# Loading attention heads over 128 partitions: three transfers a head in place of six

## The chip, the cores and the metric

The kernel runs on one core of one Trainium2 chip. The metric is the device time of one execution in microseconds (us); the time before is the median of three runs. All times from a trace are counted from the first instruction of its one profiled execution.

## The reference

One layer of a decoder: a normalised input is projected to queries, keys, values and a pooling input; 8 attention heads and 4 pooling groups are computed side by side; their outputs are projected and added; a gated MLP with a short convolution and a gated embedding follow. Sequence 2048, model width 1024, everything in 32-bit floats. The change concerns the attention alone. Of it, cut to what is computed:

```python
N_ATT_HEADS, HEAD_DIM = 8, 64
DIL_PATTERNS = ((128, 1), (512, 4), (2048, 16))      # window, dilation
for window, dil in DIL_PATTERNS:                      # banded attention in each residue class
    s = q . k  - slope[h] * distance                  # masked to the band
    m = max(s); e = exp(s - m); den = sum(e)
    o = (e . v) / den
w = den * exp(m - max over patterns); w = w / sum(w)  # mixture of the three patterns
att = sum over patterns of w * o
```

## The kernel before

**Stages.** The program runs through three functions: `phase_project` (0 to about 400 us), `phase_attention` (about 397 to 724 us) and `phase_rest` (output projection, MLP, embedding, to the end). The order on TensorE (PE) is written out by hand throughout; in the projection and the attention so are those on ScalarE (ACT), VectorE (DVE) and GpSimd (POOL). The queue of SyncE (SP), which issues most transfers, follows the order in which the program text meets them.

**High and low parts.** Each 32-bit factor is held as the sum of two parts, a high one (name ends in h) and a low one (l), which TensorE multiplies in its fast 32-bit form. A query times a key is q_high·(k_high + k_low) + q_low·(k_high + k_low). The kernel takes both key parts in one product: a head has 64 components, so a tile of 128 partitions holds the key's high parts in 64 partitions and its low parts in the other 64 (tile `ks`), and the query tile holds its 64 components twice (tile `qhh` for the high part, `qll` for the low). The sum over the 128 partitions is then the sum over components and over both key parts. Which partition holds which component is free, as long as `ks`, `qhh` and `qll` agree.

**What the projection leaves.** `phase_project` writes queries and keys to DRAM, per pair of heads 128 rows (component) by 2048 (token) of 4 bytes, so 8 KB a row: `g.qh`, `g.ql` (L370 to 371) and `g.kh`, `g.kl` (L376 to 377), and the values to `g.vn` and `g.vf` (L391).

**The attention's order.** It takes 128 steps `s`, 16 for each head (one for each block of 128 queries). `CFG["ord"]` lists what a step records and how many steps late each piece is: scores by TensorE (`near_scores` L566, `far_scores` L555; near is a block with its predecessor, far the dilated patterns), their maxima by VectorE (`near_max` L575, `far_max` L581, which read the bias tiles `nb` and `fb`), exponentials by ScalarE, a transpose, the split into high and low, and the product with the values some 6 steps later (`near_pv` L619, `far_pv` L638). `halves_sum` (L654) adds the two halves of a result: ScalarE copies one (`ev`, L659), VectorE adds (`s`, L660), and TensorE's next product `o` (L628, L642) reuses the accumulator only then.

**Head loads.** `load_qk(h)` (L500) makes head `h`'s tiles, two sets in turn by `h % 2`, and lists its transfers. Head 0's are issued at once, then the eight value tiles of pair 0 (L738 to 742). From step 1 of each head on, the next head's list is put into `queue` and one transfer is issued at each step (L749 to 753); value tiles of the next pair are issued at fixed steps in between (`V_STEPS`). A transfer first waits until the last reader of its buffer is done. For the queues of SP and ACT together, eight semaphores are used in turn, so a transfer also waits until the one eight places before it has landed.

**Mixing the patterns.** Each pair of heads ends with a mix of its patterns. In the next head, an even one, come: the pair's maxima and sums are transposed and copied (`mix_stats` L761), stored to DRAM from ScalarE's own queue one step later (`mix_stats_store`: `std` L776, `stf` L777, 32 KB each), loaded again in another layout three steps after that, from the same queue (`mix_stats_load`: `sn` L784, `sf` L788; each must wait until the store that it reads has landed), and five steps later VectorE combines them (`mix_lift` L862). From there GpSimd goes on by itself: it stores the weights (`wd`, L880), loads them spread over 128 partitions (`wb`, L891, 24 loads), multiplies (L901 to 914) and stores the result. The last pair is mixed without DRAM.

Of the kernel before, what the change touches and what calls it, by code (L numbers as in the profile page):

```python
# [11 lines left out]
F32R = mybir.dt.float32r  # L12
# [5 lines left out]
P = 128  # L18
D = 1024
KD = D // P  # L20
S = 2048
H = 8
DH = 64
# [31 lines left out]
def rdma(nc, dst, src):  # L55
    nc.sync.dma_start(fp(dst) if dst.dtype == F32R else dst, fp(src) if src.dtype == F32R else src)
# [113 lines left out]
def phase_project(tc, g, xT, w_in, pool_w, rcnt):  # L170
# [4 lines left out]
    with ExitStack() as ctx:  # L175
# [116 lines left out]
        for c, (t0, n) in enumerate(chunks):  # L292
            cs = slice(t0, t0 + n)
            final = c == len(chunks) - 1
            nxt = None
            for gi, grp in enumerate((0, 1, 2, 3) if not final else (0, 1, 3, 2)):
                if gi == 2 and not final:
                    tk.later(2, lambda st=nxt: scale(st))
                    tk.later(5, lambda st=nxt: spread_(st))
                nt = 4 if grp != 2 else n // P  # L300
                ps = [psum.tile([P, CH], F32, tag="b1", name=f"z{c}_{grp}_{j}") for j in range(nt)]
                apart = final and grp == 2
                for k in range(KD if not apart else 0):
                    if gi == 0 and c == 0 and k < KD - ACFG["nk"]:
                        norm_b(cur, k + ACFG["nk"])
                        cur.low()
                    ahead(step + ACFG["la"])
                    step += 1
                    wh, wl = held[grp, k]
                    ah, al = cur.hn[k]  # L310
                    for j in range(nt):
                        js = slice(j * P, (j + 1) * P)
                        if grp == 2:
                            mm3(nc, ps[j], ah[:, js], al[:, js], wh, wl, k == 0, k == KD - 1)
                        else:
                            mm3(nc, ps[j][:, :n], wh[:, js], wl[:, js], ah, al, k == 0, k == KD - 1)
                    tk.tick()
                    if gi == 0 and k == 6 and not final:
                        nxt = loads(c + 1)
                    if gi == 1 and not final:  # L320
                        square(nxt, k)
                    if gi == 3 and not final:
                        if k > 1:
                            nxt.low()
                        norm_a(nxt, k)
                        if k > 0:
                            norm_b(nxt, k - 1)
                    if gi == 0 and c == 0:
                        if k < 4:
                            square(cur, 2 * k)  # L330
                            square(cur, 2 * k + 1)
                        if k == ACFG["sc"]:
                            scale(cur)
                        if k == KD - 1:
                            spread_(cur)
                            inv = nxt.xs[0][:, n : 2 * n]
                            nc.scalar.copy(inv, cur.inv)
                    if gi == 0 and c > 0 and k < 2:
                        cur.low()
                        if k == 0:  # L340
                            norm_b(cur, KD - 1)
                    if c == 0 and gi == 0 and k == 4:
                        raw = small("pw_raw")
                        nc.sync.dma_start(raw.rearrange("p (a b) -> p a b", a=4), pool_w)
                        split(nc, pw_h.rearrange("p a b -> p (a b)"), pw_l.rearrange("p a b -> p (a b)"), raw)
                        nc.sync.dma_start(rc, rcnt)
                unscaled = list(range(nt)) if c == 0 and grp != 2 else []

                def by_inv():
                    if unscaled:  # L350
                        pu = ps[unscaled.pop(0)][:, :n]
                        nc.vector.tensor_tensor(pu, pu, inv, op=ALU.mult)

                by_inv()
                for j in range(nt):
                    if apart:
                        for k in range(KD):
                            js = slice(j * P, (j + 1) * P)
                            ah, al = cur.hn[k]
                            mm3(nc, ps[j], ah[:, js], al[:, js], *held[grp, k], k == 0, k == KD - 1)  # L360
                            if k % 4 == 3:
                                tk.tick()
                    by_inv()
                    pj = ps[j][:, :n]
                    pr = pj.rearrange("p (j r) -> p r j", r=4)
                    if grp == 0:
                        hi, lo = zpair("q", n)
                        nc.scalar.activation(hi, pj, AF.Copy, scale=QSCALE)
                        nc.vector.scalar_tensor_tensor(lo, pj, QSCALE, fp(hi), op0=ALU.mult, op1=ALU.subtract)
                        rdma(nc, g.qh[j][:, cs], hi)  # L370
                        rdma(nc, g.ql[j][:, cs], lo)
                    elif grp == 1:
                        hi, lo = (by_residue(z) for z in zpair("k", n))
                        nc.scalar.copy(hi, pr)
                        nc.vector.tensor_tensor(lo, pr, fp(hi), op=ALU.subtract)
                        rdma(nc, residues(g.kh[j], t0, n), hi)  # L376
                        rdma(nc, residues(g.kl[j], t0, n), lo)
                    elif grp == 2:
                        vt = sb.tile([P, H, 2, DH], F32R, tag="vt", bufs=NV, name="vt")
                        pv = ps[j].rearrange("p (h d) -> p h d", h=H)  # L380
                        if c == 0:
                            sc = cur.pw[:, j : j + 1]
                            nc.scalar.activation(vt[:, :, 0, :], pv, AF.Copy, scale=sc)
                            nc.vector.scalar_tensor_tensor(
                                vt[:, :, 1, :], pv, sc, fp(vt[:, :, 0, :]), op0=ALU.mult, op1=ALU.subtract
                            )
                        else:
                            nc.scalar.copy(vt[:, :, 0, :], pv)
                            nc.vector.tensor_tensor(vt[:, :, 1, :], pv, fp(vt[:, :, 0, :]), op=ALU.subtract)
                        for dst in (g.vn[t0 // P + j], g.vf[:, t0 // P + j]):  # L390
                            (nc.gpsimd if final else nc.sync).dma_start(  # L391
                                fp(dst.rearrange("r j h a d -> j r (h a d)")), fp(vt.rearrange("p h a d -> p (h a d)"))
                            )
                    else:
                        pool_branch(nc, g, sb, psum1, c, j, pj, t0, n, tails[j], rc, pw_h, pw_l, zpair, final)
            cur = nxt
# [7 lines left out]
def residues(t, t0, n):  # L404

    c, j0 = t0 // CH, t0 % CH // 4
    return t[:, c, :, j0 : j0 + n // 4]
# [78 lines left out]
def phase_attention(tc, g, mx, near_b, far_b):  # L486
# [5 lines left out]
    with ExitStack() as ctx:  # L492
# [8 lines left out]
        def load_qk(h):  # L501
            t = heads[h] = Shared()
            pr, e = h // 2, h % 2
            rows = slice(DH * e, DH * e + DH)
            t.qhh = sb.tile([P, S], F32R, tag=f"qhh{e}", bufs=1, name=f"qhh{h}")
            t.qll = sb.tile([P, S], F32R, tag=f"qll{e}", bufs=1, name=f"qll{h}")
            t.qr = t.qhh.rearrange("p (c r) -> p r c", r=4)
            t.qlr = t.qll.rearrange("p (c r) -> p r c", r=4)
            t.ks = sb.tile([P, NCH, 4, P], F32R, tag=f"ks{e}", bufs=1, name=f"ks{h}")
            t.nb = sb.tile([P, 256], F32, tag=f"nb{e}", bufs=1, name=f"nb{h}")  # L510
            t.fb = sb.tile([P, 512], F32, tag=f"fb{e}", bufs=1, name=f"fb{h}")
            loads = []
            for half in range(2):
                hs = slice(half * DH, half * DH + DH)
                loads.append((t.qhh[hs], g.qh[pr][rows]))
                loads.append((t.ks[hs], (g.kh if half == 0 else g.kl)[pr][rows]))
                loads.append((t.qll[hs], g.ql[pr][rows]))
            loads += [(t.fb, far_b[h]), (t.nb, near_b[h])]
            return loads

        near_v = g.vn.rearrange("n r j (p h) a d -> (r j) n p (h a d)", h=2)
        far_v = g.vf.rearrange("r (b m) j (p h) a d -> r (m j) b p (h a d)", m=4, h=2)
# [1322 lines left out]
def tile_layer(ctx, tc, xT, pT, vec, w_in, pool_w, w_out, w_up, w_down, w_gate, w_ple, near_b, far_b, rcnt, outT, upto=9):  # L1845
# [23 lines left out]

    g.qh = per(NPAIR, [P, S], F32R, "qh")  # L1870
    g.ql = per(NPAIR, [P, S], F32R, "ql")
    g.kh = per(NPAIR, [P, NCH, 4, P], F32R, "kh")
    g.kl = per(NPAIR, [P, NCH, 4, P], F32R, "kl")

    g.vn = dr.tile([NQ, 4, P // 4, H, 2, DH], F32R, tag="vn", name="vn")
    g.vf = dr.tile([4, NQ, P // 4, H, 2, DH], F32R, tag="vf", name="vf")
# [95 lines left out]
```

## Time and profile before

| what | value |
|---|---|
| time, median of 3 runs | 2456.98 us (2455.57 to 2457.58) |
| span of the profiled execution, first to last instruction | 2454.4 us |
| TensorE busy in it | 2345.7 us (96%) |
| VectorE, ScalarE, GpSimd busy | 1723.2, 1146.1, 547.3 us |
| attention, from the first score product to the last exchange of halves | 397.7 to 724.0 us |
| mean granted clock of TensorE | 0.981 |

The profiled execution's own time is its span of 2454.4 us and what lies around it; the median of the runs is 2.6 us more. The page lists busy time by engine, a chain of work that ended last (followed back from the end, each piece to what released it), groups of instructions by line, and transfers with the time from issue to landing. A wait is put down to the event that came last before it; an engine's idle time matters only where that engine, or one that waits for it, sets the end.

### The profile page before, as it was taken

What the parts mean: (1) busy time and instruction counts of PE and PEld (TensorE: products, weight loads), DVE (VectorE), ACT (ScalarE), POOL (GpSimd) and SP (SyncE); (2) the same over time, 40 slices, a digit from 0 to 9 for tenths busy, and PEclk for the clock granted to TensorE, in tenths of its full rate; (3) what the DMA queues carried; (4) which work ended last, traced back from release to release, by engine and by line L of the source; (5) the groups of instructions that cost most, each with busy time, mean ns of one, the idle gap of its engine ahead of it and who ended that gap; (6) DMA issues with size and microseconds to landing.
All of it is one profiled execution on the core that took longest, in us unless ns stands there. A gap on an engine that the chain in (4) does not pass through costs nothing.

```text
span 2454.4 us, 32544 instructions
## 1 busy us (share of the span) xinstructions
PE 2345.7 (96%) x11251; PEld 1970.6 (80%) x11251; DVE 1723.2 (70%) x2705; ACT 1146.1 (47%) x2055; POOL 547.3 (22%) x552
## 2 busy tenths in 40 slices
PE   8999999888879999999999999999999999999998
PEld 7888887787767887888888787788878888888888
DVE  6645437787774367999999989877766565755655
ACT  5423326787761125445445545444445444543332
POOL 3312221044340023344332366100020000000100
PEclk9999999898989999999999999999999999999999
DMA  7535448878747576456566778544388676654332
GB/s 240 175 133 185 146 153 249 178 173 193 181 142 260 189 253 202 161 187 211 192 197 219 260 275 272 197 145 142 125 287 287 226 255 206 215 176 158 125 100 91
DMA packets 248516, 476.06 MB, mean 194 GB/s; under 512 B 47744, under 2 KB 74176, under 8 KB 245280
## 3 DMA queue, kind: packets, MB, share of 16 engines
q1 hardware_dynamic: 199376, 385.20, 49.7%
q0 software_dynamic: 29328, 61.02, 7.4%
q10 hardware_dynamic: 19648, 27.77, 3.3%
q8 instruction: 88, 1.44, 0.3%
q14 instruction: 76, 0.62, 0.1%
HBM read 313.08 MB, written 160.73 MB: 193 GB/s over the span
## 4 chain that ended last, share of the span: by engine, by line
PE 73%; DVE 10%; DMA 7%; issue 4%; ACT 2%; POOL 0%; DVEq 0%; POOLq 0%; ACTq 0%; SPq 0%
PE ua L1319 15%; PE uc L1319 8%; PE dn L90 5%; PE dn L89 5%; PE dn L91 5%; PE ub L1319 4%; PE z L91 4%; PE z L89 4%; PE z L90 4%; PE o L89 2%; PE o L91 2%; PE o L90 2%; PE gp L89 2%; PE gp L90 2%; PE gp L91 2%
## 5 line engine op out<-in xcount | busy, mean ns | idle before, releaser
L90 PE MATMUL dn<-al,wu 128*128 128x512 f32 x616 | 240.1, 390 | 4.7 <-DVE al L85 4.7
L89 PE MATMUL dn<-ah,wu 128*128 128x512 f32 x616 | 240.1, 390 | 0.0
L91 PE MATMUL dn<-ah,wu 128*128 128x512 f32 x616 | 239.8, 389 | 0.0
L85 DVE TENSOR_TENSOR al<-ra,ah 128x512 fp32r<-128x512 f32 x154 | 105.8, 689 | 114.1 <-ACT ah L84 110.7
L89 PE MATMUL z<-hnh,wh 128*128 128x512 f32 (+1 forms) x480 | 169.9, 354 | 9.5 <-ACT hnh L252 6.0
L90 PE MATMUL z<-hnl,wh 128*128 128x512 f32 (+1 forms) x480 | 169.7, 354 | 3.4 <-DVE hnl L253 3.3
L91 PE MATMUL z<-hnh,wl 128*128 128x512 f32 (+1 forms) x480 | 169.6, 353 | 2.3 <-POOL wl L85 1.7
L84 ACT CAST ah<-ra 128x512 fp32r<-128x512 f32 x154 | 95.2, 621 | 148.2 <-PE dn L91 130.6
L90 PEld LDWEIGHTS dn<-al,wu 128*128 128x128 f32 x616 | 115.6, 188 | 30.0 <-DVE al L85 6.2
L85 DVE TENSOR_TENSOR wu<-ru,wu 128x1024 fp32r<-128x1024 f32 x88 | 136.5, 1551 | 2.4 <-ACT wu L84 2.4
L89 PEld LDWEIGHTS dn<-ah,wu 128*128 128x128 f32 x616 | 115.6, 188 | 24.3 <-ACT ah L84 0.2
L91 PEld LDWEIGHTS dn<-ah,wu 128*128 128x128 f32 x616 | 115.6, 188 | 23.9
L1319 PE MATMUL uc<-a22h,wu 128*128 128x512 f32 x352 | 116.9, 393 | 3.4 <-DVE uv L1342 3.4
L1319 PE MATMUL ua<-s1h,wu 128*128 128x512 f32 x352 | 115.8, 390 | 3.0 <-ACT ug L1546 3.0
L1319 PE MATMUL ub<-a12h,wu 128*128 128x512 f32 x352 | 117.0, 393 | 0.7 <-ACT a12h L1375 0.6
L1319 PE MATMUL ua<-s2h,wu 128*128 128x512 f32 x352 | 115.9, 390 | 0.9 <-ACT ug L1520 0.7
L1319 PE MATMUL ua<-s4h,wu 128*128 128x512 f32 x352 | 115.7, 389 | 0.5 <-ACT uv L1567 0.5
L1319 PE MATMUL uc<-s3h,wu 128*128 128x512 f32 x352 | 115.6, 389 | 0.0
L1319 PE MATMUL ua<-a11h,wu 128*128 128x512 f32 x352 | 115.5, 389 | 0.0
L85 DVE TENSOR_TENSOR wu<-rw,wu 128x512 fp32r<-128x512 f32 x149 | 101.0, 687 | 17.3 <-ACT wu L84 17.3
L89 PEld LDWEIGHTS z<-hnh,wh 128*128 128x128 f32 x480 | 94.0, 196 | 21.5 <-ACT hnh L252 6.0
L155 DVE TENSOR_TENSOR acc<-acc,sq 128x512 f32<-128x512 f32 (+1 forms) x125 | 81.1, 649 | 42.0 <-ACT sq L154 28.5
(336 smaller groups left out, 6670.3 us busy)
## 6 DMA issues: line engine op xcount, KB each, us to landing
ru<-in_w_up_dram SPq DMA_DIRECT2D x66, 512.0 KB, 4.1
wr<-in_w_in_dram SPq DMA_DIRECT2D x64, 256.0 KB, 4.2
rw<-in_w_down_dram SPq DMA_DIRECT2D x61, 256.0 KB, 4.0
nt<-h SPq DMA_DIRECT2D x56, 256.0 KB, 3.8
td<-t SPq DMA_DIRECT2D x22, 512.0 KB, 2.6
t<-td SPq DMA_DIRECT2D x22, 512.0 KB, 3.7
nt<-in_w_down_dram POOLq DMA_DIRECT2D x44, 256.0 KB, 5.4
ra<-oq0s SPq DMA_DIRECT2D x44, 256.0 KB, 3.9
```

What stands on the lines that cost most here:

```text
L84: nc.scalar.copy(hi, src)
L85: (low or nc.gpsimd).tensor_tensor(lo, src, fp(hi), op=ALU.subtract)
L89: nc.tensor.matmul(ps, wh, ah, start=first, stop=False, skip_group_check=again)
L90: nc.tensor.matmul(ps, wh, al, start=False, stop=False, skip_group_check=again)
L91: nc.tensor.matmul(ps, wl, ah, start=False, stop=last, skip_group_check=again)
L155: nc.vector.tensor_tensor(acc[:, :n], acc[:, :n], sq[:, :n], op=ALU.add)
L1319: nc.tensor.matmul(pst, x[:, ksl], y, start=first and k == 0 and n == 0, stop=k == HK - 1 and n == 2, skip_group_check=True)
```

## The change

The keys' two DRAM tensors of a pair become one, `g.kk`, with 128 rows of two parts: a row holds the component's 2048 high parts and, 8 KB on, its 2048 low parts. The projection's stores go to its halves, with the same pieces as before.

```diff
-                        rdma(nc, residues(g.kh[j], t0, n), hi)
-                        rdma(nc, residues(g.kl[j], t0, n), lo)
+                        rdma(nc, residues(g.kk[j][:, 0], t0, n), hi)
+                        rdma(nc, residues(g.kk[j][:, 1], t0, n), lo)
...
-            loads = []
-            for half in range(2):
-                hs = slice(half * DH, half * DH + DH)
-                loads.append((t.qhh[hs], g.qh[pr][rows]))
-                loads.append((t.ks[hs], (g.kh if half == 0 else g.kl)[pr][rows]))
-                loads.append((t.qll[hs], g.ql[pr][rows]))
-            loads += [(t.fb, far_b[h]), (t.nb, near_b[h])]
-            return loads
+            twice = lambda z: z[pr][rows, None].to_broadcast([DH, 2, S])
+            return [
+                (t.qhh, twice(g.qh)),
+                (t.ks.rearrange("p c r j -> p (c r j)"), g.kk[pr][rows].rearrange("d a c r j -> d a (c r j)")),
+                (t.qll, twice(g.ql)),
+                (t.fb, far_b[h]),
+                (t.nb, near_b[h]),
+            ]
...
-    g.kh = per(NPAIR, [P, NCH, 4, P], F32R, "kh")
-    g.kl = per(NPAIR, [P, NCH, 4, P], F32R, "kl")
+    g.kk = per(NPAIR, [P, 2, NCH, 4, P], F32R, "kk")
```

A head's six transfers to 64 partitions, 512 KB each, become three to 128 partitions, 1024 KB each. Partition 2d now holds component d's high key, 2d + 1 its low key, and both hold the query's component d: its DRAM row is read twice, by neighbouring partitions, within one transfer. The bytes moved are the same. A head's list is 5 transfers long in place of 8, so it is issued in 5 steps. The order of the instructions on TensorE, VectorE, ScalarE and GpSimd is the same row by row; only SP's queue changes, and with it which of the eight semaphores each transfer has.

The first place is SP's queue where head 1's loads stand, behind the values of pair 0. Before (`qhh`, `ks`, `qll` are a head's tiles, `kh` and `kl` the keys' parts in DRAM, `v` value tiles, `fb` and `nb` biases):

```order
L56 DMA v_0_3_3996<-vf 128x4x256
L56 DMA v_0_3_3998<-vn 128x4x256
L56 DMA qhh_4016<-qh_81 64x2048
L56 DMA ks_4018<-kh_89 64x2048
L56 DMA qll_4017<-ql_85 64x2048
L56 DMA qhh_4016<-qh_81 64x2048
L56 DMA ks_4018<-kl_93 64x2048
L56 DMA qll_4017<-ql_85 64x2048
L56 DMA fb_4020<-in_far_b_dram 128x512
L56 DMA nb_4019<-in_near_b_dram 128x256
```

And of the change, the same place:

```order
L56 DMA v_0_3_3989<-vf 128x4x256
L56 DMA v_0_3_3991<-vn 128x4x256
L56 DMA qhh_4009<-qh_81 128x1x2048
L56 DMA ks_4011<-kk_89 128x2048
L56 DMA qll_4010<-ql_85 128x1x2048
L56 DMA fb_4013<-in_far_b_dram 128x512
L56 DMA nb_4012<-in_near_b_dram 128x256
```

The loads stay behind all eight value loads; the second halves are gone as transfers of their own, and each of the first three is twice as large.

The second place is SP's queue in head 2, where head 3's loads stand between the last value loads of pair 1; ScalarE issues `std`, `stf`, `sn` and `sf` from its own queue in the same stretch. Before:

```order
L56 DMA qhh_4841<-qh_82 64x2048
L56 DMA v_1_2_4798<-vf 128x4x256
L56 DMA ks_4843<-kh_90 64x2048
L56 DMA v_1_2_4874<-vn 128x4x256
L56 DMA qll_4842<-ql_86 64x2048
L56 DMA qhh_4841<-qh_82 64x2048
L56 DMA v_1_3_4929<-vf 128x4x256
L56 DMA ks_4843<-kl_94 64x2048
```

And of the change, from the same load on:

```order
L56 DMA qhh_4828<-qh_82 128x1x2048
L56 DMA v_1_2_4785<-vf 128x4x256
L56 DMA ks_4830<-kk_90 128x2048
L56 DMA v_1_2_4861<-vn 128x4x256
L56 DMA qll_4829<-ql_86 128x1x2048
L56 DMA fb_4832<-in_far_b_dram 128x512
L56 DMA v_1_3_4916<-vf 128x4x256
L56 DMA nb_4831<-in_near_b_dram 128x256
```

The first five rows keep their order, with three of them twice as large; behind them the biases follow where the second halves stood. Heads 4 and 6 have the same pattern.

## The prediction, as put on record

> **What bounds the kernel now.** I read the page first, then the waits of the attention (397 to 720 us), then the chain that ended last in that stretch, and last the transfers. The page shows a kernel held by TensorE, so a change to transfers can gain only where TensorE, or what feeds it, stands still.
>
> ```profile
> PE 2345.7 (96%) x11251; PEld 1970.6 (80%) x11251; DVE 1723.2 (70%) x2705; ACT 1146.1 (47%) x2055; POOL 547.3 (22%) x552
> ```
>
> SP is held back after every head until the head's last far score is done, so its first load then marks the heads' ends (timeline of SP's queue, start and length in us; the last row is the first transfer of the next stage):
>
> ```profile
> 428.96 0.45 SPq L56 DMA_DIRECT2D qhh<-qh  x1
> ...
> 468.98 0.45 SPq L56 DMA_DIRECT2D qhh<-qh  x1
> ...
> 511.09 0.45 SPq L56 DMA_DIRECT2D qhh<-qh  x1
> ...
> 545.65 0.45 SPq L56 DMA_DIRECT2D qhh<-qh  x1
> ...
> 593.68 0.45 SPq L56 DMA_DIRECT2D qhh<-qh  x1
> ...
> 628.25 0.45 SPq L56 DMA_DIRECT2D qhh<-qh  x1
> ...
> 672.46 0.33 SPq L954 DMA_DIRECT2D rwo<-in_w_out_dram  x1
> ```
>
> Heads 1 to 6 take 40.0, 42.1, 34.6, 48.0, 34.6 and 44.2 us. Heads 3 and 5 are alike to 0.01 us and nothing waits for a transfer in them. Heads 1, 2, 4 and 6 are 5.4, 7.5, 13.4 and 9.6 us longer, 35.9 in all; in the even ones a part is the mix's own work. The waits of the attention (engine, line, waited for: us in total, times, longest) tell where transfers are in it:
>
> ```profile
> ACT ev L659 <- DMA v<-vn: 7.6, 2, 5.0
> ...
> DVE tt L577 <- PE sf L562: 4.7, 1, 4.7
> DVE lo L862 <- DMA sf<-stf: 4.7, 2, 2.5
> ACT ev L659 <- DMA stf<-sy: 3.2, 1, 3.2
> ...
> PE sn L573 <- DMA qll<-ql: 2.6, 1, 2.6
> ```
>
> The chain that ended last (start, us, what) runs through the same places:
>
> ```profile
> 409.05 8.30 DMA v<-vn
> 417.37 17.43 DMA nb<-in_near_b_dram
> ...
> 474.41 8.84 DMA stf<-sy
> ...
> 561.73 16.33 DMA sf<-stf
> ...
> 633.63 8.18 DMA stf<-sy
> 641.91 15.23 DMA sf<-stf
> ```
>
> There are three kinds. (a) Head 1's loads come late: TensorE waits 2.6 us for `qll`, VectorE 4.7 in all, since `nb` lands last, at 434.8. (b) ScalarE must wait until `std` and `stf` have landed before it can issue `sn` and `sf`, and its copy `ev` stands behind them. The row naming `v<-vn` is the same wait, as ScalarE's timeline shows: `std` goes out at 550.53, the issue of `sn` gets through at 561.24, and only then does `ev` run.
>
> ```profile
> 550.53 0.47 ACTq L776 DMA_DIRECT2D std<-sx  x1
> ...
> 561.24 0.37 ACTq L784 DMA_DIRECT2D sn<-std  x1
> ...
> 562.21 0.58 ACT L659 COPY ev<-o 64x512 f32<-64x512 f32 x1 [4.99 <-DMA v<-vn]
> ```
>
> That is 7.6 + 3.2 = 10.8 us over three pairs. (c) VectorE waits for `sf`: 4.7 us, in heads 4 and 6. In sum 4.7 + 10.8 + 4.7 = 20.2 us.
>
> These small transfers are slow because they stand among head loads (transfers: line, count, KB each, median us to landing):
>
> ```profile
> qhh<-qh SPq DMA_DIRECT2D x16, 512.0 KB, 10.7
> ...
> wb<-wd POOLq DMA_DIRECT2D x24, 256.0 KB, 9.5
> ...
> mh<-mh POOLq DMA_DIRECT2D x12, 256.0 KB, 2.7
> ...
> std<-sx ACTq DMA_DIRECT2D x3, 32.0 KB, 8.2
> stf<-sy ACTq DMA_DIRECT2D x3, 32.0 KB, 8.8
> ...
> wd<-wts POOLq DMA_DIRECT2D x3, 32.0 KB, 2.2
> ```
>
> `wd` is also a store of 32 KB, but goes out when no head load is under way: 2.2 us against 8.2 and 8.8.
>
> **The change part by part.**
>
> *The rate.* Stretches of the trace in which SP's queue carries almost nothing but one kind (last columns: share of the transfer engines, GB/s):
>
> ```profile
> 364.00:377.00 13.00, 13.00 (x59) 10.76 (x58) 2.09 (x3) 3.38 (x6) 1.90 (x5) 1.00 0.99 200
> 404.00:417.00 13.00, 12.28 (x80) 11.34 (x79) 12.12 (x39) 12.57 (x39) 0.00 (x0) 0.95 1.05 350
> 420.00:433.00 13.00, 9.59 (x64) 8.63 (x63) 9.02 (x27) 10.59 (x29) 0.00 (x0) 0.98 1.02 205
> ```
>
> The first and third are head loads to 64 partitions, the second value loads to 128: 200 and 205 GB/s against 350, all with the transfer engines full. A half load (0.524 MB) thus costs 2.6 us of all engines. A doubled one (1.049 MB) costs 3.0 at 350 and 5.2 at 200, the bounds for a transfer that the trace of before does not have. I take 3.0: it reaches all 128 partitions like the value loads. A head's six loads then cost 9.0 us in place of 15.7. The Trainium skill (SBUF — State Buffer, Door 1: The DMA port swizzle) says that a transfer's rate hangs on how many of 16 ports its partitions reach, and that 64 neighbouring ones reach half of them. By that rule a doubled load takes the 3.0; the rows agree in the rates, and no row here shows such a load.
>
> *(a) Head 1.* The value loads ahead land at 409.05 + 8.30 = 417.35 either way. Then come 3 doubled loads and the biases, 3.5 MB, 10.1 us at 350 GB/s: 427.5. TensorE is ready for them at 430.48:
>
> ```profile
> 430.48 0.36 PE L572 MATMUL sn<-ks,qhh 128*128 128x256 f32 x1 [0.45 <-DVE ptl L617]
> 433.43 0.55 PE L573 MATMUL sn<-ks,qll 128*128 128x256 f32 x1 [2.59 <-DMA qll<-ql]
> ```
>
> All 4.7 us go. What is late next is VectorE's own row of work, as in heads 3 and 5.
>
> *(b) The small stores.* Here the change has two sides. Head 2's first load, and ScalarE's first store behind it (the transfers of a stretch, with the time to landing; ScalarE's timeline):
>
> ```profile
> qhh<-qh SPq DMA_DIRECT2D x1, 512.0 KB, 4.7
> ```
>
> ```profile
> 473.86 0.51 ACTq L776 DMA_DIRECT2D std<-sx  x1
> ```
>
> SP has issued `qhh` at 468.98, a value load, `ks` and another value load by then; `stf` follows at 474.41. I take the stores to wait for what was issued before them. Before, that was two half loads and two value loads, 2.1 MB; now two whole loads and two value loads, 3.1 MB. At 350 GB/s with 2.1 us to start (that half load's 4.7, less 2.6 of data) that ends at 468.98 + 2.1 + 9.0 = 480.1. Before, `stf` landed at 474.41 + 8.84 = 483.25. The same 483.25 is reached at 3.15 MB / 12.2 us = 259 GB/s: **this edit pays above about 260 GB/s and costs below.** ScalarE waited 3.2 us, its `sn` and `sf` issued within it, so it was ready near 480.5, and the wait goes almost whole. In heads 4 and 6 GpSimd's `wb` loads run beside, so I leave 2.0 us over the three pairs: 10.8 − 2.0 = 8.8.
>
> *(c) The loads `sf`.* They are issued 2 to 4 us earlier, and behind the stores only 2.4 MB are left (one whole load, two value loads, the biases), 7 us, since the three second halves are gone. In head 4 `sf` went out at 561.73 and landed 16.33 later, at 578.06, and VectorE had waited 2.5; issued 4 us earlier, it would land near 558 + 2 + 7 = 567, long before 575.6. All 4.7 us go.
>
> *What follows a wait.* After such waits TensorE's granted clock (the third column from the right) is half, two of them shown first and one of (c) last:
>
> ```profile
> 433.00:439.00 6.00, 5.01 (x19) 4.26 (x20) 2.88 (x9) 2.10 (x6) 0.00 (x0) 0.50 1.05 215
> 484.00:490.00 6.00, 4.88 (x22) 4.79 (x23) 3.33 (x9) 3.90 (x12) 0.00 (x0) 0.50 1.08 214
> ...
> 580.00:586.00 6.00, 5.38 (x22) 4.66 (x22) 4.40 (x15) 4.40 (x13) 2.73 (x4) 0.50 0.08 11
> ```
>
> Between 0, if VectorE hides that, and the 15.7 us by which the four heads are longer beyond the 20.2 of waits, most of which is the mix's own work; I take 3, and 8 as the far end.
>
> *At nothing.* SP's 24 transfers fewer: SP waits, it isn't waited for. The stores to `g.kk`: same pieces, same count, and the first that could be late for them are head 0's loads. Those are under way from 364 to 377, with TensorE busy 13.00 of 13 us, and are first read at 397.7, which is their cover (score products, first and last start):
>
> ```profile
> L572 PE MATMUL sn<-ks,qhh x128: 222/332/562, 397.7 to 706.4; 128*128 128x256 f32 x120, 128*128 128x128 f32 x8
> ```
>
> The rows on the other four engines stand in the same order.
>
> *Sum.* 4.7 + 8.8 + 4.7 + 3 = 21.2 us. The span goes from 2454.4 to 2433; the median lies 2.6 above the span, so **2436**. After the attention TensorE takes up the saved time, since the next stage's first transfers wait for the last scores, not for a clock.
>
> **The rivals.**
>
> *Query loads at the old rate.* Each DRAM row of a query is read twice, by neighbours, and no such load is in the trace; the key's is plain. With 5.2 us for each query load and 3.0 for the key, the stores of (b) wait 5.2 + 3.0 + 3.0 = 11.2 in place of 9.0: about 1 us gained a pair, 3 in all. Head 1's loads land at 417.4 + 13.4 + 1.1 = 431.9 and keep 1.4 of the 4.7; (c) goes. 3 + 3.3 + 4.7 = 11: **2446**. For it: the one repeated load that there is, `wb`, takes 9.5 us for 256 KB where `mh` takes 2.7. Against: `wb` repeats two rows 64 times each, the query 64 rows twice. The Trainium skill (DMA: Bandwidth & Descriptors, Rules for kernel authors) says that an outer dimension of few entries confines a transfer to as many engines; `wb`'s 9.5 us fit that, and by that rule the query's 64 rows are spread fully.
>
> *The small transfers wait by turns, not by bytes.* If the engines take queues in turns, `std` waits for turns that last as long as before, a doubled load at a doubled rate. Then 10.8 stays, perhaps half of (c) goes: 4.7 + 2.3 = 7, **2450**, a part of it within 0.2%. The Trainium skill (DMA: Bandwidth & Descriptors, Queues, rings and completion order) says that each engine goes round its queues packet by packet; the 8.2 us of 32 KB speak for long turns or for a wait by bytes alike.
>
> *Slower.* If 1 MB takes 5.2 us at 128 partitions too (the rate set by the 8 KB rows, not by the partitions), the stores wait for two whole loads in place of two halves: 5.2 us more in each of three pairs, 15.6; the 4.7 of (c) vanish in it, and head 1 stays. 15.6 − 4.7 = 11 slower: **2468**. It decides below 260 GB/s. Against it: the value loads' 350.
>
> *Nothing.* The loads land sooner and the waits move to GpSimd's chain of `wb`, or the chip doesn't do what the shapes say: **2457**.
>
> **How the numbers follow.** The forecast, 2436, has a chance of 0.60; query loads at the old rate 0.11; turns 0.11 (0.02 of it within the bound); slower 0.09; nothing 0.09. About 0.2%, 4.9 us, is what a measurement of this kernel can tell from no change. Faster: 0.60 + 0.11 + 0.09 = 0.80; same 0.02 + 0.09 = 0.11; slower 0.09. The low end is all 20.2 us and 8 behind the waits, 2429. The high end takes in the first two rivals, 2452.
>
> **What would show it.** Right: head loads of 1024 KB at 300 GB/s or more in the same stretches; `std` and `stf` landing within some 6 us; no wait of `ev` for a transfer over 1 us; no wait of `lo` for `sf`; no half clock after them; heads 1, 2, 4 and 6 at 35 to 40 us. Wrong: a doubled load at over 4 us of the engines, or `std` and `stf` as late as before while the loads are fast, which would be the turns.

## The result, and the profile after

The changed kernel took **2433.56 us** (median of 4 runs, 2431.38 to 2440.15) beside 2456.28 for the kernel before (2454.95 to 2457.58). The comparison on record has a ratio of 0.9895, with a 95% interval of 0.9878 to 0.9912; the quotient of these two medians alone is 0.9907, inside it. Against two later sets of runs of the kernel before it came to 0.9901 (0.9884 to 0.9918) and 0.9895 (0.9873 to 0.9916). The profiled execution has a span of 2430.7 us in place of 2454.4.

The page of the changed kernel. VectorE, ScalarE and GpSimd are busy as long as before within 1 us; TensorE is busy 10.0 us less for the same number of products, so these ran faster (more on this below). In the second row SP's queue (packets, MB, share) takes 47.5% of the transfer engines' time, where it took 49.7% of a longer span before:

```profile
PE 2335.7 (96%) x11251; PEld 1962.2 (81%) x11251; DVE 1722.9 (71%) x2705; ACT 1145.4 (47%) x2055; POOL 548.2 (23%) x552
...
q1 hardware_dynamic: 198992, 385.20, 47.5%
```

SP's queue in the attention, the same marks of the heads' ends as before the change (start, length in us):

```profile
430.65 0.52 SPq L56 DMA_DIRECT2D qhh<-qh  x1
465.19 0.52 SPq L56 DMA_DIRECT2D qhh<-qh  x1
502.71 0.52 SPq L56 DMA_DIRECT2D qhh<-qh  x1
537.28 0.52 SPq L56 DMA_DIRECT2D qhh<-qh  x1
577.46 0.52 SPq L56 DMA_DIRECT2D qhh<-qh  x1
612.03 0.52 SPq L56 DMA_DIRECT2D qhh<-qh  x1
651.77 0.82 SPq L954 DMA_DIRECT2D rwo<-in_w_out_dram  x2
```

Heads 1 to 6 take 34.5, 37.5, 34.6, 40.2, 34.6 and 39.7 us. Against before that is 5.5, 4.6, 0, 7.9, 0 and 4.5 less: 22.4 us in all (by the unrounded starts), in just the heads that the prediction named. Besides, the attention begins 2.4 us later (400.11 in place of 397.71), head 0 is 0.7 shorter, and what follows the mark of the next stage is 3.0 shorter (1778.9 in place of 1781.9). 22.4 − 2.4 + 0.7 + 3.0 = 23.7, the difference of the spans.

Nearly half of the 22.4 us is not idle time saved but work that ran faster. Head 4 before the change (first row) and after it (second; length, then busy time and instructions of TensorE's products, weight loads, VectorE, ScalarE and GpSimd; PEclk, share of the transfer engines, GB/s):

```profile
545.65:593.68 48.03, 37.09 (x211) 33.16 (x211) 32.25 (x99) 32.47 (x90) 16.34 (x19) 0.86 0.76 181
537.28:577.46 40.18, 33.69 (x211) 30.42 (x211) 32.28 (x99) 32.48 (x90) 8.97 (x10) 0.96 0.58 197
```

The same 211 products take 3.4 us less, at a mean granted clock of 0.96 in place of 0.86, and TensorE idles 4.5 less. Over heads 1 to 6 its idle time falls by 12.4 us and the time of the same 1251 products by 10.0; the clock in heads 1, 2, 4 and 6 was 0.91, 0.92, 0.86 and 0.92 and is 1.00, 1.00, 0.96 and 0.96. The ends of products are modelled in the profile, so the split is rough.

The stretch in which head 1 is loaded (PEclk, share of the transfer engines, GB/s at the end); the three whole loads fill most of it, and the last of them lands at 427.9:

```profile
417.00:427.00 10.00, 9.20 (x63) 8.53 (x62) 8.79 (x28) 9.38 (x27) 0.00 (x0) 1.00 1.03 415
```

415 GB/s, where half loads gave 205, with the transfer engines full in both cases: a byte takes them half as long. The 350 of the value loads was a mean over a stretch whose first 3 us were not full. From 411 to 415 us, with the engines full, they ran at 385 before the change:

```profile
411.00:415.00 4.00, 3.55 (x25) 3.25 (x24) 3.69 (x12) 3.75 (x12) 0.00 (x0) 1.00 1.09 385
```

With the change, TensorE's first product of head 1 starts with no wait in its row (before: 2.59 for `qll` in the second):

```profile
431.57 0.33 PE L572 MATMUL sn<-ks,qhh 128*128 128x256 f32 x1
431.74 0.28 PE L573 MATMUL sn<-ks,qll 128*128 128x256 f32 x1
```

Of the waits for transfers that the prediction counted, this one row is left (us in total, times, longest); those of `lo` for `sf`, of `tt` and of `qll` are gone:

```profile
ACT ev L659 <- DMA stf<-sy: 3.6, 2, 2.0
```

The transfers of the attention (KB each, median us to landing) show why something is left. In head 2 the two stores land after 5.2 and 5.8 us (the two single rows), but the median over the three pairs is 7.3:

```profile
std<-sx ACTq DMA_DIRECT2D x1, 32.0 KB, 5.2
stf<-sy ACTq DMA_DIRECT2D x1, 32.0 KB, 5.8
```

```profile
std<-sx ACTq DMA_DIRECT2D x3, 32.0 KB, 7.3
stf<-sy ACTq DMA_DIRECT2D x3, 32.0 KB, 7.3
```

Behind the two waits that are left, in heads 4 and 6, TensorE's clock is half for 3.4 us each; in heads 1 to 6 these are the only such stretches:

```profile
552.80:556.20 3.40, 3.40 (x18) 3.30 (x17) 1.99 (x8) 2.38 (x7) 0.00 (x0) 0.52 0.97 309
...
627.90:631.30 3.40, 3.40 (x17) 3.35 (x17) 1.52 (x6) 2.54 (x9) 0.00 (x0) 0.52 0.85 266
```

### The profile page after: what moved, and what is told of

Its sections match the earlier page's. It is cut to its first block, busy times and chain, and to the rows that moved or that the text cites. A ratio compares the mean times of both kernels' runs of the same rounds, so it can differ in the third digit from the quotient of the medians.

```text
span 2430.7 us, 32503 instructions
## 1 busy us (share of the span) xinstructions
PE 2335.7 (96%) x11251; PEld 1962.2 (81%) x11251; DVE 1722.9 (71%) x2705; ACT 1145.4 (47%) x2055; POOL 548.2 (23%) x552
## 3 DMA queue, kind: packets, MB, share of 16 engines
q1 hardware_dynamic: 198992, 385.20, 47.5%
## 4 chain that ended last, share of the span: by engine, by line
PE 76%; DVE 9%; DMA 4%; issue 4%; ACT 3%; POOL 0%; ACTq 0%; POOLq 0%; DVEq 0%; SPq 0%
PE ua L1319 17%; PE uc L1319 8%; PE dn L91 5%; PE dn L90 5%; PE dn L89 5%; PE ub L1319 4%; PE z L89 4%; PE z L91 4%; PE z L90 4%; PE gp L89 2%; PE o L91 2%; PE o L89 2%; PE gp L91 2%; PE gp L90 2%; PE o L90 2%
## 5 line engine op out<-in xcount | busy, mean ns | idle before, releaser
L89 PE MATMUL z<-hnh,wh 128*128 128x512 f32 (+1 forms) x480 | 170.6, 355 | 11.2 <-ACT hnh L252 6.3
```

Of the source, the lines that this page charges most:

```text
L89: nc.tensor.matmul(ps, wh, ah, start=first, stop=False, skip_group_check=again)
```

## The experiments

Theory: (1) a transfer's rate hangs on which partitions it reaches; (2) the small transfers of the mix wait for the bytes issued ahead of them, and the engines' stops there are what the head loads cost. Rivals: the number or size of the transfers; the total that they cost; a small transfer's slowness of its own. Times of a kernel moved by some 0.2% between sets, so beside each time stand the heads, from the first score product of a head to that of the next (us, one profile each; head 1 of before is 39.4 by this count, not 40.0, since its first product already came late):

| kernel | head 1 | 2 | 3 | 4 | 5 | 6 |
|---|---|---|---|---|---|---|
| before | 39.4 | 42.1 | 34.6 | 48.0 | 34.6 | 44.2 |
| changed | 34.5 | 37.5 | 34.6 | 40.2 | 34.6 | 39.7 |
| six loads, every second partition | 34.6 | 37.5 | 34.6 | 37.4 | 34.6 | 37.9 |
| odd heads alone | 34.5 | 37.5 | 34.6 | 41.9 | 34.6 | 42.2 |
| even heads alone | 38.4 | 40.4 | 34.6 | 47.1 | 34.6 | 40.3 |
| before, text order, loads late | 40.3 | 37.5 | 34.6 | 40.1 | 34.6 | 42.0 |
| changed, text order, loads late | 34.6 | 37.5 | 34.6 | 37.7 | 34.6 | 37.5 |
| changed, `wb` by rows | 34.6 | 37.5 | 34.6 | 37.5 | 34.6 | 37.5 |

**Six loads again, spread over every second partition.**

```diff
...
+            for half in range(2):
+                hs = slice(half, P, 2)
+                loads.append((t.qhh[hs], g.qh[pr][rows]))
+                loads.append((t.ks[hs], g.kk[pr][rows][:, half]))
+                loads.append((t.qll[hs], g.ql[pr][rows]))
...
```

> The changed kernel, but each head is again loaded by six transfers of 512 KB; each half goes to every second of the 128 partitions in place of 64 neighbouring ones. If it is the spread over all partitions that makes the loads fast, the six run at 380 GB/s or more in the stretch in which head 1 is loaded (before: 205, changed: about 416), heads 1, 2, 4 and 6 stay within 1 us of 34.5, 37.5, 40.2 and 39.7 us, and the time is 2434 (2431 to 2440). If it is the number of transfers or their size, the rate stays near 205 GB/s, the heads take 40, 42, 48 and 44 us as before, and the time is 2456. If it is the length of what one partition gets at one go (neither differs here), nothing is told.

2431.01 us (2428.29 to 2436.41), ratio 0.988 (0.986 to 0.990). Head 1's loads, in the same columns as above:

```profile
417.00:425.00 8.00, 7.18 (x48) 6.55 (x47) 6.92 (x21) 7.38 (x22) 0.00 (x0) 1.00 0.99 409
```

Six transfers of 512 KB to 64 partitions each, as before, but at 409 GB/s in place of 205. For the rate neither number nor size matters, nor that a transfer reaches only 64 partitions: it is which 64. The Trainium skill (SBUF — State Buffer, Door 1: The DMA port swizzle) has neighbours 0 to 63 on half of the ports; by the formula given there every second partition reaches all of them, and the trace agrees. The small stores even land sooner than behind three whole loads (median 4.6 and 6.0 us in place of 7.3 and 7.3), and heads 4 and 6 are 2.7 and 1.9 shorter.

**The same three transfers, in two blocks.**

```diff
-            twice = lambda z: z[pr][rows, None].to_broadcast([DH, 2, S])
+            twice = lambda z: z[pr][None, rows].to_broadcast([2, DH, S])
...
-                (t.ks.rearrange("p c r j -> p (c r j)"), g.kk[pr][rows].rearrange("d a c r j -> d a (c r j)")),
+                (t.ks.rearrange("p c r j -> p (c r j)"), g.kk[pr][rows].rearrange("d a c r j -> a d (c r j)")),
```

> The changed kernel, but the three loads of a head fill the partitions in two blocks: the source runs first over the two copies (query) or over high and low (key) and then over 64 rows, so 64 neighbouring partitions come from one entry of the outermost dimension, in place of 64 entries with two neighbours each. Same bytes, same rows of 8 KB, same 128 partitions. If only the partitions that a transfer reaches count, it is the changed kernel: 2434, head loads at about 400 GB/s. If the outermost dimension of the source (2 entries) says how many of the 16 transfer engines take part, a load of 1 MB goes through 2 of them, takes 20 us or more (the wb loads, 256 KB with two outermost entries, take 8 us alone), three of them 60 us in place of 8, which is more than a head's 35 us: attention up by some 25 us in each of 7 heads, about 2600.

2742.26 us in one run, 309 more than the changed kernel. While a head's loads are alone under way:

```profile
500.00:510.00 10.00, 0.00 (x0) 0.00 (x0) 0.00 (x0) 0.00 (x0) 0.00 (x0) 0.50 0.13 54
```

All compute engines stand still and 0.13 of the transfer engines are busy, which is 2 of 16 (0.125), at 54 GB/s: 1.049 MB takes 19.4 us. The same bytes to the same 128 partitions, in another order of loops, are nearly eight times slower. The Trainium skill (DMA: Bandwidth & Descriptors, Rules for kernel authors) states that an outermost dimension of fewer than 16 entries confines a transfer to at most as many engines, and the trace agrees with it. It is why the order of loops matters in this change. `wb` has two outermost entries and shows the same: from 648 to 651 us in the changed kernel, with three `wb` loads under way and nothing else, 37.0% of the transfer engines are busy, which is 6 of 16, or 2 for each. The forecast of 2600 was too low: it took some 60 us for a head, and the heads took 62 to 83 (first score products, as in the table). What beside the loads fills them was not followed up.

**Only odd heads, and only even heads.** In `load_qk`, heads with `h % 2 == 0` (first) or `== 1` (second) get the six old transfers from `g.kk`:

```diff
+            if h % 2 == 0:
+                loads = []
...
+                    loads.append((t.ks[hs], g.kk[pr][rows][:, half]))
```

> The changed kernel, but only heads 1, 3, 5 and 7 are loaded by three transfers; heads 0, 2, 4 and 6 by six to 64 neighbouring partitions each. Heads 3, 5 and 7 are the ones whose loads stand ahead of the small stores and loads of the mix, in heads 2, 4 and 6, and head 1 is the one whose loads came late. If the gain comes from there, nearly all of it stays: 2436 (2432 to 2441), std and stf landing in 5 to 8 us as in the changed kernel. If it comes from the total that the head loads cost, half of the loads keep about half of the gain: 2445 (2442 to 2449).

> The changed kernel, but only heads 0, 2, 4 and 6 are loaded by three transfers; heads 1, 3, 5 and 7 by six to 64 neighbouring partitions each. It is the counterpart to the kernel with the odd heads alone. If the gain comes from the loads that stand beside the mix's small transfers and from head 1's, little is left: 2455 (2450 to 2458), with std and stf landing in 8 to 11 us, ScalarE's copy ev waiting some 10 us in all and VectorE's lo for sf some 5. If it comes from the total, about half: 2445 (2442 to 2449).

Odd heads alone: 2437.42 us (2430.80 to 2439.19), ratio 0.9899 (0.9878 to 0.9919). Even heads alone: 2450.80 (2448.36 to 2457.65), ratio 0.9957 (0.9944 to 0.9970). So the odd heads, whose loads stand where the waits are, carry most, and the total of the loads is not what counts. But the even heads alone are not without effect: heads 1 to 6 are 7.5 us shorter, 3.9 of it in head 6, and the odd heads alone are 4.2 longer than with both. The even heads' loads run beside GpSimd's `wb`; in the kernel before, the last two `wb` loads ahead of head 4 land 9.8 and 12.8 us after its mark, with even heads alone 0.2 before and 2.5 after it. That they thereby leave the small stores freer is read from these traces; the last experiment takes it up.

**The kernel before, with head loads later.** Two kernels. In the first only the step at which the next head's list is put into `queue` is moved; in the second SP is also taken from the scheduler and keeps the order of the text.

```diff
-                    if n == 1 and h + 1 < H:
+                    if n == (7 if h in (2, 4, 6) else 1) and h + 1 < H:
```

```diff
-        with tc.manual_schedule(engines=set(EN.values())):
+        with tc.manual_schedule(engines={*EN.values(), mybir.EngineType.SP}):
```

> The kernel before, with its six loads of 512 KB to 64 partitions, but in heads 2, 4 and 6 the next head's loads start at step 7 of the head in place of step 1, behind the mix's small stores and loads. Their rate stays at 200 GB/s. If what matters is only what stands ahead of the small transfers, std and stf land in 2 to 4 us, the waits (b) of 10.8 us and (c) of 4.7 us go and some of the half clock with them, while head 1's wait (a) stays: 2440 (2436 to 2445). If the stores are slow for another reason than the head loads ahead of them, the waits stay and the time is 2456. If the later loads come too late for the next head, TensorE waits at the starts of heads 3, 5 and 7, and the time is 2456 or more in spite of the stores.

> The kernel before, with its six loads of 512 KB to 64 partitions at 200 GB/s, but SP's queue now stands in the order of the text, and in heads 2, 4 and 6 the next head's loads come at step 7, behind all value loads of the pair (moving the step alone left SP's queue nearly as it was). If the small stores are slow only because of the head loads issued ahead of them, std and stf land in 2 to 5 us, the waits (b) and (c) go, heads 2, 4 and 6 take 37 to 38 us, and the time is 2441 (2437 to 2446); head 1's wait (a) stays. If the stores are slow for another reason, the waits stay and the time is 2456. If the loads come too late for the next head, heads 3, 5 and 7 begin with a wait and the gain is lost there.

The first: 2460.07 us, ratio 0.9996 (0.9982 to 1.001), no change. It did not do what it was to do. SP's queue of that kernel in head 2, which began at 471.85:

```profile
470.94 0.45 SPq L56 DMA_DIRECT2D qhh<-qh  x1
472.05 0.36 SPq L56 DMA_DIRECT2D v<-vf  x1
472.46 0.51 SPq L56 DMA_DIRECT2D ks<-kh  x1
```

The head loads still start first. The section on the kernel before says that SP follows the text; that is wrong. The lists of engines set by hand leave SP out, a scheduler puts its transfers in order, and a step in the text moves them little.

The second does move them. Its queue in head 2 has the pair's value loads first, and the head loads 14 us into the head, where before the first went out ahead of it:

```profile
472.08 0.36 SPq L56 DMA_DIRECT2D v<-vf  x1
475.84 0.36 SPq L56 DMA_DIRECT2D v<-vn  x1
482.60 0.36 SPq L56 DMA_DIRECT2D v<-vf  x1
485.27 0.36 SPq L56 DMA_DIRECT2D v<-vn  x1
485.68 1.32 SPq L56 DMA_DIRECT2D qhh<-qh  x1
```

```profile
std<-sx ACTq DMA_DIRECT2D x3, 32.0 KB, 5.1
stf<-sy ACTq DMA_DIRECT2D x3, 32.0 KB, 5.0
...
wd<-wts POOLq DMA_DIRECT2D x3, 32.0 KB, 9.9
```

With the slow half loads as they were, the stores land after 5 us, no wait of `ev` for a transfer is left and 1.3 us of `lo` (before: 10.8 and 4.7), and head 2 takes 37.5 us. Head 4 takes 40.1, as in the changed kernel, but for another reason: here the wait of `lo` is left in it, there one of `ev`. So most of (b) and (c) hangs on the head loads issued ahead of the small transfers, as the prediction had it. The time misses its forecast of 2437 to 2446: 2451.11 us, from 2442.84 to 2467.60 (12 runs), ratio 0.9978 (0.9957 to 0.9998). The profile is of one of the fast ones; it shows the collision that moved: `wd` now lands after 9.9 us, and head 6 begins with a wait.

```profile
620.77 0.36 PE L573 MATMUL sn<-ks,qll 128*128 128x256 f32 x1 [1.82 <-DMA qll<-ql]
```

Neither place of these loads that was run is a good one at 200 GB/s; why single runs lie 25 us apart is left open.

**The changed kernel, with head loads later**, by both edits above, and the changed kernel once more beside it.

> The changed kernel, with SP's queue in the order of the text and, in heads 2, 4 and 6, the next head's loads at step 7. What the changed kernel still loses there (heads 4 and 6 at 40.2 and 39.7 us, beside 37.5 for head 2; 3.6 us of ScalarE's copy ev waiting for stf) goes if whole loads ahead of the small stores are its cause: heads 4 and 6 at 37.5, 4.9 us less, ratio 0.0020 under that of the changed kernel run beside it. If the rest is the mix's own or GpSimd's work, nothing changes: within 1.5 us of it.

> The changed kernel unchanged, beside the others on the same chip, as what they are measured against: ratio to before 0.9895 as in its first comparison (0.988 to 0.991).

2433.18 us (2429.62 to 2433.82), ratio 0.9896 (0.9879 to 0.9913), beside 2433.87, ratio 0.9901 (0.9884 to 0.9918). The stores land after 4.0 and 3.7 us, heads 4 and 6 are at 37.7 and 37.5. The heads did what was expected, but 4.7 us (3.5 against the neighbour's own 38.8 and 39.9) can't be seen in the time: from the start of head 7 to the end the profiles of these kernels range from 1773.7 to 1784.8 us, for the same work.

**Both ways at once, and the spread loads once more**, with the changed kernel beside them.

> Both at once: six loads to every second partition, and SP's queue in the order of the text with the next head's loads at step 7 in heads 2, 4 and 6. If each of the two alone already takes all that head loads cost in the attention (heads 2, 4 and 6 were 37.4 to 37.9 us in either), nothing adds up: heads 2, 4 and 6 at 37.5, the time within 0.2% of the changed kernel's, 2431 (2428 to 2435). If a wait is left that neither takes alone, heads 2, 4 and 6 fall below 37 us.

> Six loads to every second partition, as before, now beside the changed kernel on one chip. By the attention alone it should be 4.5 us faster than the changed kernel's first profile (heads 4 and 6 at 37.4 and 37.9 in place of 40.2 and 39.7); the other stages moved by as much from run to run without a cause in the kernel. If the attention's gain shows, ratio to the changed kernel 0.998 or 0.9985; if the other stages cover it, 0.999 to 1.001.

> The changed kernel unchanged, as the measure for the two kernels beside it: 0.990 of the kernel before (0.988 to 0.992), 2434.

Both: 2432.14 us (2426.81 to 2433.43), ratio 0.9886 (0.9866 to 0.9907), heads 2, 4 and 6 all at 37.5: nothing adds up, and 37.5 is what such a head takes without waits for transfers. Spread loads: 2429.68 (2426.26 to 2432.78), ratio 0.988 (0.9858 to 0.9903), heads 4 and 6 at 37.8 and 37.6. Changed: 2434.72 (2426.36 to 2438.25), ratio 0.9895 (0.9873 to 0.9916), heads 4 and 6 at 40.4 and 39.9. In this one set that has both, the means of the runs differ by 3.6 us with a standard error of 2.2. So the heads show the gain of the spread loads a second time, and the time does not show it.

**`wb` by rows.**

```diff
-        q.dma_start(w, g.wd[pr][2 * a : 2 * a + 2, None, cs].to_broadcast([2, DH, CH]))
+        for e in range(2): q.dma_start(w[e * DH : e * DH + DH], g.wd[pr][2 * a + e : 2 * a + e + 1, cs].to_broadcast([DH, CH]))
```

> The changed kernel with its head loads as they are, but each of GpSimd's wb loads (256 KB, two weight rows spread over 64 partitions each, source's outermost dimension 2) is split into two of 128 KB, one row each, with 64 entries outermost. In the changed kernel the value loads issued ahead of heads 4 and 6 stay under way for some 10 us while two wb loads are, and the small stores behind them land after 7.4 us. If it is wb's two transfer engines that hold them back, a pair of wb loads lands in 2 to 4 us in place of 9.4, the stores in 4 to 6, heads 4 and 6 take 37.5 to 38.5 us in place of 40.2 and 39.7, and the time is 2430 (2427 to 2434). If the head and value loads ahead are the cause by their bytes alone, heads 4 and 6 stay at 39 to 40.5 and the time at 2434; then wb may land faster without being felt, since GpSimd is waited for by nobody in these heads.

2430.30 us (2427.55 to 2437.15), ratio 0.9877 (0.9859 to 0.9896). First the value load issued ahead of head 4 in the changed kernel, then the same with `wb` by rows, then that kernel's `wb`:

```profile
v<-vf SPq DMA_DIRECT2D x1, 512.0 KB, 11.3
```

```profile
v<-vf SPq DMA_DIRECT2D x1, 512.0 KB, 3.3
```

```profile
wb<-wd POOLq DMA_DIRECT2D x48, 128.0 KB, 3.6
```

No wait of `ev` for a transfer is left and heads 4 and 6 are at 37.5, with the head loads untouched. So what the changed kernel still loses there hangs on the `wb` loads. They are under way for some 9 to 12 us ahead of head 4, each on 2 of the 16 transfer engines, and loads that use all engines land late with them. Whether the stores wait for this alone is not separated: with faster `wb` loads GpSimd also gets on sooner, and two stores of 256 KB (`mh`, `ml`) that it issues at 544.05 and 544.63 in the changed kernel, beside `std` and `stf`, go out before head 4. By heads this kernel is level with the one that has both ways at once, and no other is shorter; by time it is not told apart from the spread loads.

## Why the prediction was right, point by point

- **The rate** of a doubled load was taken as 350 GB/s from the value loads; it is 415, so 1.049 MB takes 2.5 us of all engines and not 3.0. The 350 was itself too low for the value loads, which run at 385 once the engines are full. The break-even of 260 was far off, and with it the slower case.
- **(a)** went whole. The loads were forecast to land at 427.5 and TensorE to be ready at 430.5; they land at 427.9 (`qll`) to 428.8 (`nb`), though the attention began 2.4 us later, and TensorE starts at 431.57. The head is 5.5 us shorter by SP's marks: on TensorE 2.9 of idle time and 2.6 of faster products, since the half clock behind the wait is gone too.
- **(b)** in head 2: from SP's first load to the landing of `stf` the sum gave 480.1 − 468.98 = 11.1 us. Measured: issue at 465.19, `stf` at 470.62 + 5.8 = 476.4, so 11.2. That the two agree so well is partly luck: at the measured 415 GB/s the same bytes give 2.1 + 7.6 = 9.7. Nor do the stores wait for all that was issued ahead of them: in heads 4 and 6 `stf` lands at 550.3 and 624.7, and the value load issued just ahead of it at 552.4 and 626.8. In heads 4 and 6 the term was mis-sized: 3.6 us are left over the three pairs and not 2.0. The prediction named `wb` as the reason for what it left and gave no sum for it; the last experiment shows that the wait goes when the `wb` loads are fast.
- **(c)** went whole.
- **What follows a wait** was set at 3 us. Of the 22.4 us, the waits account for 4.7 + (10.8 − 3.6) + 4.7 = 16.6, so 5.8 went with them; both errors, −1.6 and +2.8, nearly cancel, which is luck. These waits are of several engines. On TensorE itself the 22.4 is 12.4 of idle time and 10.0 of faster products, so the clock is a larger part of the gain than the 3 us made it, and a part of the 16.6 was no idle time of TensorE.
- **At nothing.** The stores to `g.kk`: the attention starts 2.4 us later than before, but kernels with the stores of before started at 398.5 and 399.4, and others with `g.kk`, the two-block kernel left out, from 397.8 to 403.6. No shift by the stores can be told from this.
- **After the attention** the time was taken up, and 3.0 us more: less than the 11.1 by which that stretch ranges.
- **The rivals.** Query loads at the old rate: no, the stretch at 415 GB/s holds two of them. Turns: not as it was put, with the stores as late as before; in head 2 they land after 5.2 and 5.8 us in place of 8.2 and 8.8, and `ev` waits 3.6 us in place of 10.8. That the queues share the engines by turns to some degree is not excluded, since the stores overtake a value load issued ahead of them; no run separates this from a wait by bytes. Slower, and nothing: no.
- **The marks.** Met: 300 GB/s, no wait of `lo`, and nearly the heads, at 34.5 to 40.2 where 35 to 40 was said. Not met: stores within 6 us in heads 4 and 6, no wait of `ev` over 1 us, and so no half clock at all.

## What to carry to other kernels

Look at which partitions a transfer reaches and at the outermost loop of its source before its size or count: here 64 neighbouring partitions cost half the rate, and two outermost entries seven eighths of it. A big transfer that no engine waits for costs by what is queued behind it, so look for the small transfer that an engine waits for, and ask what was issued ahead of it, and on which transfer engines. A small gain behind a large one may be plain in one stretch of the trace and still not be seen in the time.

## What the hardware showed that was not expected

- Doubled loads ran at 415 GB/s, faster than the value loads' 385 with full engines, although each query row is read twice.
- With two transfers of 256 KB under way, each on 2 of the 16 transfer engines, a 512 KB load took 11.3 us to land; with those bytes split by rows, in transfers that land after 3.6 us, it took 3.3.
- TensorE gained 10.0 us of the 22.4 not by idling less but by running the same products at a higher granted clock.
- The same code after the attention ranged over 11.1 us, and the start of the attention over 5.9, from kernel to kernel (the two-block kernel left out), where heads without waits repeat within 0.05 us.
